# Start-up of a pooling-mixer trunk: who evicts the first fold, where the row factors stand, which queue stores the first block, and when the later weights are formed

## The chip, the cores and the metric

The kernel runs on one core of a Trainium2 chip. The metric is the time on the device, in microseconds (us), as the median of several runs. One more execution of each kernel was recorded by the hardware profiler; all rows of a profile come from that one execution.

## What is computed

The reference runs one layer (DEPTH is 1), so only the pooling mixer is used, on 4096 tokens of width 1024 in float32:

```python
h = x
normed = rms_norm(h, norm_w)                    # over the 1024 channels
u, gate = split(normed @ pool_in_w, 2)          # 1024 -> 2 x 1024
ug = u in 4 groups of 256 channels
pooled[g] = trailing_mean(ug[g], (2, 4, 8, 16)[g]) - ug[g]
mixed[g] = pooled[g] @ group_w[g] + group_b[g]
h = h + (mixed * scale * silu(gate)) @ pool_out_w
return rms_norm(h, final_norm_w)
```

## The kernel before, in words

**Three stages.** Pooling is linear, so the group map is folded into the input weights first: `fold` multiplies a transposed slice of the value half of `pool_in_w` by `group_w` and scales the product by the norm weight. It is called for 4 chunks of rows in each of two halves q of the value columns. Stage "a" (4 blocks b of 1024 tokens) multiplies the normalised input by the folded weights of half q = 0, stage "b" by those of q = 1, both with the gate columns of their half; stage "o" multiplies by `pool_out_w`, adds x and does the final norm.

**Seven products for eight.** Each block's product is a 2 by 2 block product done with seven multiplications (Strassen-Winograd). They are called P1 to P7 and run in the order P1, P2, P6, P7, P5, P4, P3. Each is 48 matmuls in stage a. Their left and right sides are sums and differences of quarters: of the input ("11", "12", "21", "22"), and of the weights.

**Each float32 operand is split in two.** `split` makes a rounded high part on ScalarE (`copy`) and the rest on VectorE (`sub`), both as fp32r; `mm3` multiplies three of the four pairs. A product thus needs 4 operand tiles written by ScalarE and VectorE (the weights `w[i]`, kept for all blocks, and the operands `op0` to `op3`, two for each product, so that a product's operands are split while the product before it runs).

**The start.** This is where the change lies. TensorE warms up, folds half q = 0 (chunks 0 to 3), folds half q = 1, and begins the products of block 0. Meanwhile:

- `fold` ends with one eviction of a PSUM bank for each of two halves of a chunk, on ScalarE (L296), in both q. With the first half's results VectorE and ScalarE make the weights of P1 (`split_scaled`, L205/L206) and of P6 (`second_side`, L886).
- The row factors 1/rms of block 0 come in two halves of 512 tokens. ScalarE squares and sums 4 tiles of rows (`square_row`, L315), `stats` (L322, `rsqrt` L186 to L190) makes the factors, and `spread_rs` puts them across the partitions: a high and low part, two products with an identity tile on VectorE (L339, into the tile of the weights of P7), two matmuls with ones (L346), a copy into `rstd`. The input quarters are multiplied by `rstd` (`normalize`, L148).
- The results of the second fold are stored to DRAM (`wvd`, L895) from SyncE's queue, between the loads of the input. They are read back much later.
- `split_in` (L435) splits a product's operands and stores some of the quarters to DRAM for stage b (`sd`, L379), from ScalarE's queue. For P6 it also forms the quarter sum for P3 (`form_s4`).
- `rest_of_first` makes the weights of P5, P4 and P3 in the steps n = 2, 3 and 4 (P6, P7, P5) of the main loop, ahead of the forming and splitting of the operands of the steps to come.

**What sets the order.** The program is recorded in Python order and a scheduler places the instructions of each engine by priority; `tc.high_priority()` lifts what is recorded inside it, `tc.issue_after` holds a piece back. Each engine then runs its list strictly in order. A DMA takes one of 8 completion counters in turn, so that the ninth DMA of SyncE and ScalarE waits until the first of them has landed; DMAs that GpSimd issues have a set of 8 counters of their own. Buffers for quarters come from pools (`st`, `vt`, and the still unused weight tiles `early`, `early5`) by age; a buffer that is still being stored can't be written again.

Tiles of the start that the text below names: `op_85`, `op_86` hold P1's, P6's and P5's operands, `op_87`, `op_88` P2's, P7's and P4's. `vt_102`, `vt_103` are the quarter "12" of block 0, `st_93`, `st_94` the quarter "21", `vt_105`, `vt_106` the quarter "22", which is loaded last.

Of the kernel before, what the change touches and what calls it, by code (L numbers as in the profile page):

```python
# [12 lines left out]
AF = mybir.ActivationFunctionType  # L13
ALU = mybir.AluOpType
# [16 lines left out]
P1, P2, P3, P4, P5, P6, P7 = range(1, 8)  # L31
# [29 lines left out]
def kernel(  # L61
# [32 lines left out]
    nc = tc.nc  # L94
# [7 lines left out]
    banks = [psum.tile([P, H], F32, tag=f"bank{i}", name=f"bank{i}") for i in range(8)]  # L102
# [35 lines left out]
    def give(ap):  # L138
        next(p for p in (st, vt, early, early5) if id(ap) in p.used).give(ap)
# [13 lines left out]
    def split(dst, src):  # L153
# [5 lines left out]
    norm_c = [colt[:, k : k + 1] for k in range(NK)]  # L159
# [5 lines left out]
    wvd = [dram.tile([P, 2, H], F32, name=f"wvd{k}") for k in range(4)]  # L165
# [6 lines left out]
        for i in range(P1, P7 + 1)  # L172
    }
    sd = [
        {
            i: [dram.tile([P, 2, H], F32, name=f"sd{b}_{i}_{h}") for h in range(2)]
            for i in (P1, P2, P7, P4)
        }
        for b in range(NB)
    ]  # L180
# [100 lines left out]
            )  # L281
        return r

    def fold(q, k, g, r, ps2, o):

        for kk in range(2):
            for j in range(2):
                for t in range(2):
                    nc.tensor.matmul(  # L289
                        ps2[kk][:, j * 256 : (j + 1) * 256],  # L290
                        r[:, kk, 2 * j + t, :],
                        g[:, 2 * j + t, :],
                        start=(t == 0),
                        stop=(t == 1),
                    )
            last = nc.scalar.activation(o[:, kk], ps2[kk], AF.Copy, scale=norm_c[k + kk])  # L296
        give(r)
        return last

# [4 lines left out]
    def load_row(b, half, j, pool=None):  # L304
        row = b * TB + (1 - half) * H
        rows = x[row : row + H, :].rearrange("(p j) d -> p j d", j=4)
        u = take("p (a b) -> p a b", pool, a=1)
        nc.sync.dma_start(out=u[:, 0], in_=rows[:, j, :])
        held[b, half, j] = u
# [10 lines left out]
    def stats(b, half):  # L320
        ms = small.tile([P, 4], F32, tag="ms", name=f"ms{b}_{half}")
        nc.vector.tensor_scalar(  # L322
            out=ms, in0=sums[b, half], scalar1=1.0 / D, scalar2=EPS, op0=ALU.mult, op1=ALU.add
        )
        tmp = small.tile([P, 4], F32, tag="tmp", name=f"tmp{b}_{half}")
        rs = small.tile([P, 4], F32, tag="rs", name=f"rs{b}_{half}")
        rsqrt(rs, tmp, ms)
        return rs
# [4 lines left out]
    def spread_rs(half, rs):  # L333

        hl = small.tile([P, 2, 4], F32R, tag="hl", name=f"hl{half}")
        split(hl, rs)
        r = w[P7][0]
        for s in range(2):
            nc.vector.tensor_tensor(  # L339
                out=r[:, s, 0].rearrange("p (a j) -> p a j", j=4),  # L340
                in0=ident.rearrange("p a b -> p (a b)")[:, 0:P].unsqueeze(2).to_broadcast([P, P, 4]),
                in1=hl[:, s].bitcast(F32).unsqueeze(1).to_broadcast([P, P, 4]),
                op=ALU.mult,
            )
        for s in range(2):
            nc.tensor.matmul(  # L346
                banks[7], ones, r[:, s, 0], start=s == 0, stop=s == 1, skip_group_check=True
            )
        if half == 0:
            rstd[0] = take()  # L350
        copy(rstd[0][:, half], banks[7])
# [18 lines left out]
        turn[0] += 1  # L370
        return t.rearrange(pattern, **sizes)

    def split_halves(us, saved=None):
        ts = []
        for h, u in enumerate(us):
            t = next_op("p (s a b) -> p s a b", s=2, a=2)
            split(t, u)
            if saved is not None:
                nc.scalar.dma_start(out=saved[h], in_=u)  # L379
            ts.append(t)  # L380
        return ts

# [46 lines left out]
    def normalize_a2(b):  # L429
        for h in range(2):  # L430
            normalize(b, 1, xs[b]["21"][h])
            normalize(b, 1, xs[b]["22"][h])
        give(rstd.pop(b))

    def split_in(q, b, i):  # L435
        s = xs[b]
        key = {P1: "11", P2: "12", P6: "2", P7: "21", P5: "11", P4: "22", P3: "12"}[i]
        t = split_halves(s[key], None if q else sd[b].get(i))
        if i == P6:
            form_s4(b)  # L440
        if i not in (P1, P2, P6):
            for u in s.pop(key):
                give(u)
        return t

    def form_s4(b):
        for u, s2 in zip(xs[b]["12"], xs[b]["2"]):
            sub(u, u, s2)
# [335 lines left out]
    def form(n):  # L784
        kind, b, i = step(n)
        if kind in ("a", "b"):
            form_in(kind == "b", b, i)
# [15 lines left out]
    def run(n, between=None):  # L803
        kind, b, i = steps[n]
        sets = sets_of(kind, b)
        if kind == "o":
            product_out(i, split_up.pop(n), sets, n == len(steps) - 1)
            evict_o(b, i, sets)
        else:
            product_in(i, split_up.pop(n), sets, i == P1, between)  # L810
            evict_in(b, 0 if kind == "a" else 1, i, sets)
# [30 lines left out]
    gw, ru, g0 = [None] * 2, {}, []  # L842
# [15 lines left out]
    for n, (h, k) in enumerate(chunks):  # L858
        if k < 4:
            o = v0[h] = take(pool=early)  # L860
        else:
            o = v1[h] = take()
        fold(0, k, gw[0], ru[0, k], banks[2 * (n % 2) : 2 * (n % 2) + 2], o)
        if n == 0:
            ru[1, 0] = load_wut(1, 0)
            load(0)
        elif n == 1:
            for hh in range(2):
                split_scaled(w[P1][hh], g0[hh], pair(norm_c, hh, 0))
        elif n == 2:  # L870
            for j in range(4):
                square_row(0, 0, j)
            rs = stats(0, 0)
    give(gw[0])
    for h, k in chunks[1:]:
        ru[1, k] = load_wut(1, k)
# [15 lines left out]
    for n, (h, k) in enumerate(chunks):  # L892
        o = take(pool=early if n < 2 else early5)
        last = fold(1, k, gw[1], ru[1, k], banks[2 * (n % 2) : 2 * (n % 2) + 2], o)
        nc.sync.dma_start(out=wvd[k // 2], in_=o)  # L895
        give(o)
        if n == 0:
            spread_rs(0, rs)
            form(0)
            split_step(0)  # L900
            second_side(0)
        elif n == 2:
            behind = last.ins
    give(gw[1])
    load(2)
    with tc.issue_after(behind):
        for j in range(4):
            square_row(0, 1, j)
    rs = stats(0, 1)
    run(0, lambda: spread_rs(1, rs))  # L910
    give(ident)
    form(1)
    split_step(1)
# [44 lines left out]
    def advance(what, n, f, reach):  # L958
        while at[what] + 1 < len(steps) and at[what] + 1 <= n + reach(*steps[at[what] + 1]):
            at[what] += 1  # L960
            f(at[what])
# [20 lines left out]
    for n in range(2, len(steps)):  # L982
        kind, b, i = steps[n]
        ahead = kind == "a" and b + 1 < NB
        keep[0] = 5 if kind == "b" and b == NB - 1 else 3
        advance("load", n, load, load_reach)
        if ahead:
            rows, squares = row_plan(b)
            for half, rs in scales.items():
                store_rs(b + 1, half, rs)  # L990
                load_rstd(b + 1, half)
            scales.clear()
            for j in squares.get(i, ()):
                with tc.issue_after(evicted[0]):
                    square_row(b + 1, j // 4, j % 4)
                if j % 4 == 3:
                    scales[j // 4] = stats(b + 1, j // 4)
            for j in rows.get(i, ()):
                load_row(b + 1, j // 4, j % 4, early if b == 0 and i == P6 else None)
        if kind == "a" and b == 0:  # L1000
            rest_of_first(n)
        if kind == "a" and b > 0 and i == P1:
            normalize_a2(b)
        form(n + 2)
        advance("split", n, split_step, split_reach)
        pool_due(n)
        run(n)
        if kind in ("a", "b"):
            pool_later(n)
            if kind == "a":  # L1010
                pool_due(n)
            if b == NB - 1:
                load_w(wbd if kind == "a" else wod, i)
            if i == P5:
                if kind == "a" and b in (1, 2):
                    make_wb(b - 1)
                elif kind == "b" and b in (1, 2):
                    make_wo(b - 1)
            if kind == "b" and b == NB - 1 and i == P3:
                f = take("p (a b) -> p a b", a=2)  # L1020
                nc.sync.dma_start(
                    out=f.rearrange("p a b -> p (a b)"), in_=final_w.partition_broadcast(P)
                )
                fw.append(f)
# [52 lines left out]
```

## Time and profile before

| what | us |
|---|---|
| median of 3 runs (lowest, highest) | 977.49 (976.59, 979.3) |
| the profiled execution, whole | 976.22 |
| its span, first to last instruction | 974.4 |
| TensorE busy in the span | 952.1 |
| VectorE busy | 741.5 |
| ScalarE busy | 456.7 |

The profile has these views, used below: the page (busy time of each engine), the waits (which line of an engine waited for what, in total, how often, the longest), the timeline of one engine (start, us, engine, line, operation, tiles, count, and in brackets the idle time before with what ended it), the groups of instructions (busy us, mean ns of one), and windows (busy time and DMA traffic in stretches). In a timeline, a group "x48" spans all of its instructions. Tiles are named there without their numbers. Instructions of VectorE and ScalarE overlap by about 0.1 us: two of 1.23 us take 2.36.

### The profile page before, as it was taken

The numbers are of one execution on the slowest core, as the hardware profiler recorded it, in microseconds if no ns is written. First come the engines' busy times: TensorE is split into PE (matmuls) and PEld (weight loads), VectorE is DVE, ScalarE is ACT, GpSimd is POOL, SyncE is SP. The second block draws the span as 40 slices with busy tenths as digits, with TensorE's granted clock in tenths as the row PEclk, the third lists the DMA queues.
The fourth block names the chain that finished last, engine by engine and source line by source line (L and its number), as shares of the span: only waits on it lengthen the run. The fifth ranks groups of instructions, "written<-read, shape, count | busy, mean of one in ns | idle before, by whom it ended". The sixth has DMA issues, their size and how long they took to land.

```text
span 974.4 us, 11068 instructions
## 1 busy us (share of the span) xinstructions
PE 952.1 (98%) x4190; PEld 786.3 (81%) x4190; DVE 741.5 (76%) x899; ACT 456.7 (47%) x687; POOL 0.2 (0%) x4
## 2 busy tenths in 40 slices
PE   8898999999999999999999999999999999999996
PEld 7777888878877888888888888888888888888885
DVE  3688893887699694497598499589987677677675
ACT  6658447437455454335444535553414324334333
POOL 0000000000000000000000000000000000000000
PEclk9999999999999999999999999999999999999999
DMA  9985675877885624114704723645646446356022
GB/s 336 369 313 152 229 262 168 323 270 237 316 289 205 230 104 153 44 43 152 302 34 145 274 89 130 223 163 181 224 161 236 118 164 216 109 195 214 23 87 87
DMA packets 68933, 184.35 MB, mean 189 GB/s; under 512 B 6928, under 2 KB 24464, under 8 KB 68880
## 3 DMA queue, kind: packets, MB, share of 16 engines
q1 hardware_dynamic: 63552, 165.81, 49.1%
q10 hardware_dynamic: 5328, 17.84, 4.6%
q8 instruction: 33, 0.54, 0.2%
q14 instruction: 20, 0.16, 0.1%
HBM read 116.50 MB, written 67.12 MB: 188 GB/s over the span
## 4 chain that ended last, share of the span: by engine, by line
PE 83%; DVE 6%; DMA 6%; ACT 3%; issue 1%; SPq 0%
PE bank L455 81%; DMA rd<-rs 1%; PE bank L289 1%; DMA st<-rd 1%; DMA vt<-in_xt 1%; DMA wbd<-vt 1%; DMA wbd<-st 1%; DVE w L145 1%; DVE op L145 1%; DVE vt L148 1%; DVE vt L145 1%; ACT st L315 1%; PE bank L835 1%; DVE vt L142 1%; DVE st L145 1%
## 5 line engine op out<-in xcount | busy, mean ns | idle before, releaser
L455 PE MATMUL bank<-op,w 128*128 128x512 f32 x2688 | 612.4, 390 | 9.3 <-DVE op L145 5.9
L455 PEld LDWEIGHTS bank<-op,w 128*128 128x128 f32 x2688 | 503.9, 188 | 117.2 <-DVE op L145 8.0
L455 PE MATMUL bank<-w,op 128*128 128x512 f32 (+1 forms) x1356 | 305.0, 387 | 0.0
L455 PEld LDWEIGHTS bank<-w,op 128*128 128x128 f32 x1356 | 253.0, 188 | 52.0
L151 ACT ACTIVATE op<-st 128x1024 fp32r<-128x1024 f32 x121 | 127.5, 1056 | 144.7 <-PE bank L455 116.2
L145 DVE TENSOR_TENSOR op<-st,op 128x1024 fp32r<-128x1024 f32 x121 | 147.2, 1223 | 58.8 <-ACT op L151 58.5
L142 DVE TENSOR_TENSOR vt<-vt 128x1028 f32<-128x1028 f32 (+6 forms) x72 | 88.1, 1235 | 1.1 <-DMA wbd<-vt 0.9
L151 ACT ACTIVATE op<-vt 128x1024 fp32r<-128x1024 f32 x45 | 47.6, 1058 | 73.2 <-PE bank L455 64.0
L142 DVE TENSOR_TENSOR st<-bank,st 128x512 f32<-128x512 f32 x76 | 51.9, 688 | 35.5 <-PE bank L455 33.3
L151 ACT ACTIVATE vt<-bank 128x512 f32<-128x512 f32 x94 | 54.8, 594 | 39.8 <-PE bank L455 33.7
L142 DVE TENSOR_TENSOR vt<-bank,vt 128x512 f32<-128x512 f32 (+1 forms) x85 | 57.0, 680 | 15.1 <-PE bank L455 8.7
L145 DVE TENSOR_TENSOR op<-vt,op 128x1024 fp32r<-128x1024 f32 x45 | 55.0, 1223 | 16.8 <-ACT op L151 16.6
L145 DVE TENSOR_TENSOR w<-st,w 128x1024 fp32r<-128x1024 f32 x32 | 39.1, 1225 | 23.7 <-ACT w L151 23.4
L151 ACT ACTIVATE w<-st 128x1024 fp32r<-128x1024 f32 x32 | 33.7, 1058 | 36.6 <-PE bank L455 28.7
L151 ACT ACTIVATE bank<-bank 128x512 f32<-128x512 f32 x48 | 27.9, 582 | 45.0 <-PE bank L455 32.5
L145 DVE TENSOR_TENSOR st<-st,st 128x1024 f32<-128x1024 f32 x38 | 46.2, 1224 | 2.7 <-issue 1.4
L148 DVE TENSOR_TENSOR st<-st,st 128x1024 f32<-128x1024 f32 (+1 forms) x22 | 25.4, 1174 | 22.0 <-DMA st<-rd 20.7
L151 ACT ACTIVATE st<-bank 128x512 f32<-128x512 f32 x36 | 20.7, 596 | 21.7 <-PE bank L455 10.4
L536 DVE SCALAR_TENSOR_TENSOR vt<-vt,vt 128x1024 f32<-128x1024 f32 x24 | 29.4, 1227 | 0.1
L289 PE MATMUL bank<-early,early 128*128 128x256 f32 x128 | 28.2, 380 | 1.1 <-ACT st L315 1.1
L289 PEld LDWEIGHTS bank<-early,early 128*128 128x128 f32 x128 | 24.3, 191 | 4.8 <-ACT st L315 1.5
L142 DVE TENSOR_TENSOR st<-st,st 128x1024 f32<-128x1024 f32 x21 | 25.4, 1227 | 0.1
(105 smaller groups left out, 407.9 us busy)
## 6 DMA issues: line engine op xcount, KB each, us to landing
st<-in_x SPq DMA_DIRECT2D x32, 512.0 KB, 4.4
st<-sd SPq DMA_DIRECT2D x29, 512.0 KB, 4.7
vt<-in_x SPq DMA_DIRECT2D x27, 512.0 KB, 5.0
st<-in_xt SPq DMA_DIRECT2D x20, 512.0 KB, 5.4
sd<-st ACTq DMA_DIRECT2D x20, 512.0 KB, 6.5
st<-yd SPq DMA_DIRECT2D x19, 512.0 KB, 3.8
yd<-st SPq DMA_DIRECT2D x17, 512.0 KB, 3.0
out<-st SPq DMA_DIRECT2D x17, 512.0 KB, 4.6
```

The source lines that it names most:

```text
L142: nc.vector.tensor_tensor(out=dst, in0=a, in1=b, op=ALU.add)
L145: nc.vector.tensor_tensor(out=dst, in0=a, in1=b, op=ALU.subtract)
L148: nc.vector.tensor_tensor(out=dst, in0=a, in1=b, op=ALU.mult)
L151: return nc.scalar.activation(dst, src, func)
L289: nc.tensor.matmul(ps2[kk][:, j * 256 : (j + 1) * 256], r[:, kk, 2 * j + t, :], g[:, 2 * j + t, :], start=(t == 0), stop=(t == 1),)
L315: nc.scalar.activation(u[:, 0], u[:, 0], AF.Square, accum_out=sums[b, half][:, j : j + 1])
L455: nc.tensor.matmul(ps, a, b, start=start and n == 0, stop=stop and n == 2, skip_group_check=True)
L536: nc.vector.scalar_tensor_tensor(out=s[:, :, at : at + H], in0=s[:, :, at : at + H], scalar=1.0 / win, in1=v[:, :, HIST:], op0=ALU.mult, o ...
L835: nc.tensor.matmul(banks[4 + c % 4], warm[:, 0:P], warm, start=True, stop=True, skip_group_check=True)
```

## The change

Five edits, all in the start:

1. The evictions of the first fold (q = 0) go to VectorE, as a `tensor_scalar` multiplication by the same column.
2. `stats` and `spread_rs` of block 0 are recorded under `tc.high_priority()`, in both halves; the first `spread_rs`, with the forming and splitting of P1's operand and the first `second_side`, is recorded after the second chunk of the second fold (n == 1) in place of the first.
3. The stores of the second fold (`wvd`) are issued by GpSimd in place of SyncE.
4. The stores of block 0's quarters (`sd`) are issued by GpSimd in place of ScalarE.
5. In the main loop at n = 2, the splitting of P7's operand comes first, then `form_s4` of block 0 and the forming for P5, and only then `rest_of_first`; at later n `rest_of_first` also stands behind forming and splitting. `normalize_a2` keeps its place ahead of them.

```diff
-    def fold(q, k, g, r, ps2, o):
+    def fold(q, k, g, r, ps2, o, on_vector=False):
...
-            last = nc.scalar.activation(o[:, kk], ps2[kk], AF.Copy, scale=norm_c[k + kk])
+            if on_vector:
+                last = nc.vector.tensor_scalar(
+                    out=o[:, kk], in0=ps2[kk], scalar1=norm_c[k + kk], scalar2=None, op0=ALU.mult
+                )
+            else:
+                last = nc.scalar.activation(o[:, kk], ps2[kk], AF.Copy, scale=norm_c[k + kk])
...
-                nc.scalar.dma_start(out=saved[h], in_=u)
+                (nc.gpsimd if by_pool else nc.scalar).dma_start(out=saved[h], in_=u)
...
-        t = split_halves(s[key], None if q else sd[b].get(i))
-        if i == P6:
+        t = split_halves(s[key], None if q else sd[b].get(i), b == 0)
+        if i == P6 and (q or b):
             form_s4(b)
...
-        fold(0, k, gw[0], ru[0, k], banks[2 * (n % 2) : 2 * (n % 2) + 2], o)
+        fold(0, k, gw[0], ru[0, k], banks[2 * (n % 2) : 2 * (n % 2) + 2], o, True)
...
-            rs = stats(0, 0)
+            with tc.high_priority():
+                rs = stats(0, 0)
...
-        nc.sync.dma_start(out=wvd[k // 2], in_=o)
+        nc.gpsimd.dma_start(out=wvd[k // 2], in_=o)
         give(o)
-        if n == 0:
-            spread_rs(0, rs)
+        if n == 1:
+            with tc.high_priority():
+                spread_rs(0, rs)
...
-    rs = stats(0, 1)
-    run(0, lambda: spread_rs(1, rs))
+    with tc.high_priority():
+        rs = stats(0, 1)
+
+    def spread_second():
+        with tc.high_priority():
+            spread_rs(1, rs)
+
+    run(0, spread_second)
...
-        if kind == "a" and b == 0:
-            rest_of_first(n)
         if kind == "a" and b > 0 and i == P1:
             normalize_a2(b)
-        form(n + 2)
+        if n > 2:
+            form(n + 2)
         advance("split", n, split_step, split_reach)
+        if n == 2:
+            form_s4(0)
+            form(n + 2)
+        if kind == "a" and b == 0:
+            rest_of_first(n)
```

## The prediction, on record before the changed kernel ran

> **What bounds the kernel now.** First the page, for the share of each engine; then the waits of TensorE over the whole run.
>
> ```profile
> PE 952.1 (98%) x4190; PEld 786.3 (81%) x4190; DVE 741.5 (76%) x899; ACT 456.7 (47%) x687; POOL 0.2 (0%) x4
> ...
> PE bank L455 <- DVE op L145: 5.9, 5, 3.3
> PE bank L346 <- DVE w L339: 2.8, 1, 2.8
> PE bank L455 <- ACT op L151: 2.3, 2, 1.6
> PE bank L835 <- DVE op L833: 1.4, 1, 1.4
> PE bank L289 <- ACT st L315: 1.1, 1, 1.1
> PE bank L455 <- ACT bank L151: 1.1, 1, 1.1
> ```
>
> TensorE is busy 952.1 of the span's 974.4 us. The change takes no matmul away, so it can win only from the 22.3 us in which TensorE stands. 14.6 us of them are the six waits here; the rest is the last eviction and store, which is not touched. Where the waits lie is read from TensorE's timeline of the start:
>
> ```profile
> 7.47 13.97 PE L289 MATMUL bank<-early,early 128*128 128x256 f32 x64
> 22.54 3.69 PE L289 MATMUL bank<-early,early 128*128 128x256 f32 x16 [1.10 <-ACT st L315]
> 29.06 1.10 PE L346 MATMUL bank<-w,w 128*128 128x512 f32 x2 [2.83 <-DVE w L339]
> 30.01 10.52 PE L289 MATMUL bank<-early,early 128*128 128x256 f32 x48
> 40.18 7.40 PE L455 MATMUL bank<-op,w 128*128 128x512 f32 x31
> 47.42 0.39 PE L346 MATMUL bank<-w,w 128*128 128x512 f32 x1
> ...
> 48.10 0.39 PE L346 MATMUL bank<-w,w 128*128 128x512 f32 x1
> 48.32 14.44 PE L455 MATMUL bank<-op,w 128*128 128x512 f32 x63
> 64.40 1.21 PE L455 MATMUL bank<-op,w 128*128 128x512 f32 x4 [1.63 <-ACT op L151]
> 66.29 11.17 PE L455 MATMUL bank<-op,w 128*128 128x512 f32 x48 [0.68 <-ACT op L151]
> 80.78 1.45 PE L455 MATMUL bank<-op,w 128*128 128x512 f32 x5 [3.32 <-DVE op L145]
> ```
>
> Two places count. Ahead of the first spread (29.06) TensorE stands 1.10 + 2.83 = 3.93 us: **stall A**. Before P6 (64.40, 66.29) and P7 (80.78) it stands 1.63 + 0.68 + 3.32 = 5.63 us: **stall C**. Between them, at the second spread (47.42, 48.10), it does not stand: **place B**. The remaining 3.7 us of the waits lie after 200 us, in stages the change does not edit.
>
> **Edit 1, half of the evictions to VectorE, and edit 2, the first factors: stall A.** VectorE's and ScalarE's timelines, and the waits of that stretch:
>
> ```profile
> 25.24 0.75 DVE L886 SCALAR_TENSOR_TENSOR st<-st,colt,early 128x512 f32<-128x512 f32 x1
> ...
> 27.11 1.22 DVE L145 TENSOR_TENSOR w<-st,w 128x1024 fp32r<-128x1024 f32 x1 [0.65 <-ACT w L151]
> ...
> 28.32 1.29 DVE L339 TENSOR_TENSOR w<-early,hl 128x512 fp32r<-128x512 f32 x2
> 26.02 1.06 ACT L151 ACTIVATE w<-st 128x1024 fp32r<-128x1024 f32 x1 [1.62 <-DVE st L886]
> L296 ACT ACTIVATE early<-bank,colt 128x512 f32<-128x512 f32 x12 | 7.9, 681 | 6.5 <-PE bank L289 6.4
> L142 DVE TENSOR_TENSOR vt<-bank,vt 128x512 f32<-128x512 f32 (+1 forms) x85 | 57.0, 680 | 15.1 <-PE bank L455 8.7
> L206 DVE SCALAR_TENSOR_TENSOR w<-st,colt,w 128x512 fp32r<-128x512 f32 x6 | 4.2, 750 | 11.9 <-ACT w L205 11.9
> ```
>
> No row shows a `tensor_scalar` from PSUM on VectorE. The nearest, L142 from a bank, is 0.68 us; one SBUF operation on 512 columns is 0.75; I take 0.69. Eight of them put 5.5 us on VectorE, which idles 11.9 us there behind L205, and take 8 x 0.681 = 5.4 us off ScalarE. But the first factor isn't bound by ScalarE's evictions alone. In the changed program's order VectorE does, from the last bank of the fold on (7.47 + 13.97 = 21.44): eviction 0.69, the low part of P6's first weights 1.14 (two of these take 2.36, so one step is 1.14), the mean (0.1), the difference for the second weights 1.14, reciprocal (0.1), two L886 steps 1.33 and the small steps: 26.0. That is where the last L886 ends now (25.24 + 0.75 with the factor's small steps between). From there the chain is unchanged: ScalarE's high part of those weights (26.02 to 27.08), VectorE's low part, only then the high and low part of the factor and L339. High priority has not lifted the factor past these weights. So **stall A stays**, within 0.4 us either way; the 1.10 before it merges with it. One fold matmul (two records of 13.97 / 64 = 0.22 us) now stands between the two spread matmuls, which take 1.10 for 2 x 0.39, and fills 0.3 us of that gap: **-0.3**.
>
> **Place B, the second factor.** ScalarE's and VectorE's rows:
>
> ```profile
> 42.19 1.05 ACT L315 ACTIVATE vt<-vt 128x1024 f32<-128x1024 f32 x1
> 43.14 0.19 ACT L315 ACTIVATION_READ_ACCUMULATOR vt<-vt 128x1 f32 x1
> 43.80 0.20 ACT L186 ACTIVATE tmp<-ms 128x4 f32<-128x4 f32 x1
> 46.19 1.29 DVE L339 TENSOR_TENSOR w<-early,hl 128x512 fp32r<-128x512 f32 x2
> ```
>
> Now the last square ends at 43.3 and TensorE has the factor at 47.4. In the new order more stands in the chain: ScalarE's high part of `op_87` (0.95) before the square root, which ends at 44.6; VectorE's low part of `op_87` until 45.6, reciprocal and two small steps to 46.2, low part of `op_88` 1.14, two low parts of P2's weights 0.66 each around the last small steps, then the factor's low part: L339 at 49.0 to 50.2, 2.7 later. TensorE's spread matmul now stands behind 38 of P1's matmuls, not 31: at 14.44 / 63 = 0.229 each it is reached at 40.18 + 38 x 0.229 = 48.9. It waits to 49.6 and the second to 50.2, with one matmul between: **+0.9 us of new wait**. Behind it in TensorE's queue stand P1's last 9 and P2; nothing else waits for them. If the cover of the 7 further matmuls were gone, it would be 2.5.
>
> **Edits 3 and 4, stores from GpSimd: the loads.** SyncE's waits and timeline, DMA windows (us, busy of each engine, clock, DMA share, GB/s), the chain, and the wait on `vt_103`:
>
> ```profile
> SPq L199 <- DMA sd<-st: 8.4, 1, 8.4
> 39.69 3.62 SPq L895 DMA_DIRECT2D wvd<-early  x4
> 28.00:32.00 4.00, 2.83 (x12) 2.24 (x13) 2.71 (x5) 0.92 (x2) 0.00 (x0) 1.00 1.03 410
> 36.00:40.00 4.00, 4.00 (x20) 3.51 (x20) 2.45 (x2) 2.97 (x6) 0.00 (x0) 1.00 0.85 342
> 40.00:43.40 3.40, 3.40 (x17) 2.82 (x16) 0.12 (x2) 3.40 (x8) 0.00 (x0) 1.00 0.79 263
> 46.48 11.70 DMA vt<-in_xt
> 38.27 1.23 DVE L148 TENSOR_TENSOR vt<-vt,st 128x1024 f32<-128x1024 f32 x1 [0.67 <-DMA vt<-in_xt]
> sd<-st ACTq DMA_DIRECT2D x20, 512.0 KB, 6.5
> ```
>
> SyncE stood 8.4 us at a load because its counter belonged to a quarter's store that ScalarE had issued late; then came four `wvd` issues, 3.62 us. Both leave SyncE's queue, and the last quarter's four loads are issued some 12 us sooner. They do not land 12 us sooner: the same 4 MB of stores stay ahead in traffic, and DMA runs at 410 GB/s when full. What is won is the hole: (68 x 4.0 + 147 x 3.4) / 410 = 1.9 us. The last load, landed at 46.48 + 11.70 = 58.18, comes at about 56.3, the one before it (512 KB, 1.28 us) at 55.0. ScalarE's 8 issues cost it nothing on the path.
>
> **Edit 5 and stall C.** VectorE's rows before P6:
>
> ```profile
> 54.56 2.36 DVE L148 TENSOR_TENSOR st<-st,st 128x1024 f32<-128x1024 f32 x2
> ...
> 65.02 2.36 DVE L145 TENSOR_TENSOR op<-early,op 128x1024 fp32r<-128x1024 f32 x2
> 79.49 2.37 DVE L145 TENSOR_TENSOR op<-st,op 128x1024 fp32r<-128x1024 f32 x2
> ```
>
> The last row is P7's operand, now behind P5's weights and P4's sums (65.02 to 79.49): the 3.32 us. In the new order it stands beside P6's. After L339 at 50.2: P2's second weights 1.32, P7's first weights 1.14, so the second quarters' `normalize` starts at 52.7, not 54.56. Four of these, four sums, P7's second weights, the low parts of `op_87` and `op_85`: 11 x 1.14 = 12.5, to 65.3 if no load is late. `vt_105` would be wanted at 53.8 and lands at 55.0: +1.2, so 65.4 for `op_87` and 66.5 for `op_85`. TensorE leaves P2 at 48.32 + 14.44 + 0.9 = 63.7, does P6's first 4 matmuls (0.9), waits 0.8 for `op_87`, does 4, and waits 0.3: **1.1 us in place of 5.63** (0 with early loads; 3.0 if the last load still lands at 58.18, which puts all 1.9 us later). P7's second half (`op_88`, 2.3 us after `op_87`) is wanted 11 us later. Late next are P5's operand and weights, moved behind: four more operations of 1.14 (`form_s4`, P5's sums), then P5's weights (four steps of 1.14 and two pairs of 0.66, 7.2 in all), then `op_85`, ready at about 82; TensorE wants it 21.9 us after P6's start, at 86.7. Cover 5 us.
>
> **Sum.** -0.3 (A) + 0.9 (B) - 5.63 + 1.1 (C) = **-3.9 us**. The profiled execution, 976.22 (974.4 and 1.8 around), goes to 972.3. It lies 1.27 below the median of 977.49, so the median goes to **973.6**.
>
> **Rivals.** (1) *The stores crowd the loads.* For: the last quarter's loads and the stores are now in flight together from about 29 us on. Against: DMA is full (1.03) now as well. Place: VectorE's mean for the second factor stands behind `normalize` of `vt_103`, now landed at 38.25. It is needed by 43.4 - 1.2 = 42.2. Three `wvd` ahead of it, served first, are 3 x 1.28 = 3.8 us: 42.1, the edge. Every us beyond is one of TensorE's at B. At 2.4 us beyond, the gain is 1.5: **976.0**, no change. The Trainium skill ("DMA: Bandwidth & Descriptors", section "Issuing engines are not separate DMA queues") says that transfers of all issuing engines end on the same 16 engines and interleave. That is this rival; the 410 GB/s agree.
>
> (2) *GpSimd's stores come out slowly*, the slower side. GpSimd has 12 DMAs in one queue and issued none before. VectorE's `form_s4` writes into `vt_102` and `vt_103` at 67.7 (52.7 + 13 x 1.14), which must be stored by then; they are ready at 38 to 42 us, and such a store takes 6.5 us now. It decides from 67.7 + 5 (cover) = 73 on. Were they issued only when VectorE pauses, they would land after 67.7 + 6.5 = 74, `st_93` (P6's eviction waits for its store) 6.5 later, behind it on ScalarE P5's weights: some 8 us, **981.6** (973.6 + 8). The Trainium skill ("SBUF — State Buffer", section "SBUF: two separate sides") warns of just this: a DMA from GpSimd waits while VectorE holds their common port in a two-port mode. Its section "Who interferes with whom" narrows it: operations with two SBUF inputs take only the read side. The rows between 28 and 66 us are nearly all TENSOR_TENSOR and SCALAR_TENSOR_TENSOR, so by the second sentence little is lost; no row here shows a DMA from GpSimd.
>
> (3) *The factors come sooner than worked out* (evictions shorter than 0.69, small steps between): stall A down by up to 0.4, B and C to nothing, later waits less: up to 6.5 us, **971.0**.
>
> **How the numbers follow.** Of this kernel's time, 0.3% (2.9 us) can be told from no change: 974.6 and 980.4 are the bounds. The forecast with rival 3 has 0.63 (of that rival 3: 0.08), all faster; rival 1, gains of 0 to 2.9, 0.28; rival 2 and other losses 0.09. The range runs from 970.8 (a little beyond rival 3) to 977.5 (a gain of nothing), leaving out rival 2 and a little on either side.
>
> **What would show it.** In the new profile: the first L346 still at 29 to 29.5 with about 4 us of wait (else A is wrong); a wait of 0.5 to 1.5 us at the second L346, near 50 (over 2: rival 1); at P6 at most 3 us in all, and none at P7; the last `vt` load landed at 55 to 57; GpSimd's stores of `vt_102` and `vt_103` landed before 60 (after 70: rival 2). The forecast is wrong if waits beyond 100 us grow from 3.7 to over 6.

## The result: 972.25 us, and the profile after

| what | before | after |
|---|---|---|
| median of 4 runs each (lowest, highest), us | 977.93 (976.59, 979.3) | 972.25 (971.78, 973.14) |
| after as a share of before, 95% interval | | 0.9952 [0.9935, 0.9969] |
| the profiled execution; its span, us | 976.22; 974.4 | 973.14; 971.0 |
| TensorE's waits up to 135 us; from there to 303 us | 11.00; 3.67 | 6.24; 5.47 |

The changed kernel is faster by 0.5%; the interval leaves out 1. The ratio here and those further down are as recorded with the runs; the quotient of the two medians is 0.9942 (5.7 us) and lies within the interval. The prediction said 973.6, from 970.8 to 977.5. The last row adds up the bracketed idle times of TensorE's timeline, the opening 1.4 us included; after 303 us TensorE waits no more in either kernel. The page and the waits of after:

```profile
PE 951.5 (98%) x4190; PEld 786.4 (81%) x4190; DVE 745.6 (77%) x907; ACT 452.2 (47%) x679; POOL 6.7 (1%) x16
...
PE bank L460 <- DVE op L145: 4.7, 4, 2.1
PE bank L351 <- DVE w L344: 3.5, 2, 2.9
```

TensorE's busy time is the same (952.1 before); VectorE has the eight evictions, GpSimd its twelve DMA issues. The wait of 2.3 us behind ScalarE's operands is gone from the list. Where the rest lies is read from TensorE's timeline:

```profile
22.38 3.69 PE L289 MATMUL bank<-early,early 128*128 128x256 f32 x16 [1.10 <-DVE st L297]
29.00 0.50 PE L351 MATMUL bank<-w,w 128*128 128x512 f32 x1 [2.94 <-DVE w L344]
29.34 0.59 PE L289 MATMUL bank<-early,early 128*128 128x256 f32 x2
...
39.74 9.00 PE L460 MATMUL bank<-op,w 128*128 128x512 f32 x38
49.29 0.50 PE L351 MATMUL bank<-w,w 128*128 128x512 f32 x1 [0.56 <-DVE w L344]
...
50.23 78.99 PE L460 MATMUL bank<-op,w 128*128 128x512 f32 x346
129.40 66.95 PE L460 MATMUL bank<-op,w 128*128 128x512 f32 x294 [0.18 <-DVE op L145]
...
198.24 12.30 PE L460 MATMUL bank<-op,w 128*128 128x512 f32 x53 [1.89 <-DVE op L145]
211.50 74.00 PE L460 MATMUL bank<-op,w 128*128 128x512 f32 x325 [0.96 <-ACT bank L151]
287.56 11.18 PE L460 MATMUL bank<-op,w 128*128 128x512 f32 x48 [2.06 <-DVE op L145]
```

The reader is to see three things. Stall A is there as before (1.10 + 2.94). Place B has a small new wait, 0.56. And the row "x346" runs from 50.23 to 129 us without a bracket: both P6 and P7 lie in it, so stall C is gone whole. The waits near 200 and 290 us are longer than they were.

VectorE's timeline shows why C is gone:

```profile
52.22 1.22 DVE L148 TENSOR_TENSOR st<-st,st 128x1024 f32<-128x1024 f32 x1
53.55 1.23 DVE L148 TENSOR_TENSOR vt<-vt,st 128x1024 f32<-128x1024 f32 x1
...
55.83 1.22 DVE L148 TENSOR_TENSOR vt<-vt,st 128x1024 f32<-128x1024 f32 x1
...
62.64 1.22 DVE L145 TENSOR_TENSOR op<-st,op 128x1024 fp32r<-128x1024 f32 x1
63.78 2.36 DVE L145 TENSOR_TENSOR op<-early,op 128x1024 fp32r<-128x1024 f32 x2
66.05 1.22 DVE L145 TENSOR_TENSOR op<-st,op 128x1024 fp32r<-128x1024 f32 x1
...
79.13 1.22 DVE L145 TENSOR_TENSOR op<-st,op 128x1024 fp32r<-128x1024 f32 x1
```

The four `normalize` follow each other with no load in brackets: the loads of the last quarter (L393) have landed. The last of them, in after (its issue, and the time from there to its landing), puts that at 36.0 + 18.8 = 54.8 us, 3.3 us sooner than before (58.18):

```profile
L393 SPq DMA_DIRECT2D vt<-in_xt x1: 328/328/328, 36.0 to 36.0; - x1
...
DMA to landing us min/median/max: 18.8/18.8/18.8
```

The first row of `op<-st` (62.64) is `op_87`, P7's operand: TensorE's list has four of P7's matmuls behind the first four of P6, so it is the first low part that is needed there, and it is ready at 63.86. P7's second one (66.05) now also stands beside P6's, not at 79.49. What moved behind it, P5's operand, is the row at 79.13: early enough, since no wait follows.

The stores from GpSimd: the issues (column after the bar: busy us, mean ns) and their landing (KB, median us from issue to landing), then the two stretches in which DMA was not full before:

```profile
L901 POOL DMA_DIRECT2D wvd<-early x4 | 2.3, 565 | 33.1 <-ACT early L301 31.2 <-DMA vt<-in_xt 1.9
L384 POOL DMA_DIRECT2D sd<-vt x4 | 2.1, 533 | 15.2 <-DVE vt L148 14.9 <-issue 0.3
```

```profile
wvd<-early POOLq DMA_DIRECT2D x4, 512.0 KB, 7.7
sd<-st POOLq DMA_DIRECT2D x4, 512.0 KB, 6.6
sd<-vt POOLq DMA_DIRECT2D x4, 512.0 KB, 7.5
```

```profile
36.00:40.00 4.00, 4.00 (x20) 3.51 (x20) 1.23 (x1) 3.33 (x7) 1.06 (x2) 1.00 1.03 413
40.00:43.40 3.40, 3.40 (x17) 2.78 (x16) 1.36 (x3) 3.40 (x7) 1.07 (x2) 1.00 1.03 415
```

The hole is filled (342 and 263 GB/s before), and the stores land in 6.3 to 9.6 us (the medians are 6.6 to 7.7); the median of `sd<-st` from ScalarE's queue, over the whole kernel before, is 6.5. A second stretch, which the prediction did not count, was not full before either; before, then after:

```profile
48.00:52.00 4.00, 4.00 (x20) 3.30 (x19) 2.39 (x4) 2.44 (x5) 0.00 (x0) 1.00 1.00 362
```

```profile
48.00:52.00 4.00, 3.44 (x15) 2.34 (x14) 3.53 (x6) 3.71 (x7) 0.00 (x0) 1.00 1.03 419
```

The new wait at B is read from the chain of work (start, length, what) in that stretch:

```profile
29.77 17.83 DMA st<-in_in_w
...
47.62 0.72 ACT w L205
48.35 0.10 ACT hl L151
...
48.47 0.16 DVE hl L145
48.63 0.61 DVE w L344
...
49.29 0.50 PE bank L351
```

The second factor's high part (`hl`, ScalarE) stands behind the scaling of P2's second weights (L205), and that waits for their load until 47.6. The prediction had put the whole wait on VectorE's list. That load was issued 9.5 us sooner than before (29.77, not 39.22) and yet landed 4 us later (47.60, not 43.61): it is now in flight together with the stores, and without them (ns, below) it lands at 40.4.

### The profile page after: what moved, and what is told of

It reads as the page before. It is cut to its first block, busy times and chain, and to the rows that moved or that the text cites. A ratio compares the mean times of both kernels' runs of the same rounds, so it can differ in the third digit from the quotient of the medians.

```text
span 971.0 us, 11079 instructions
## 1 busy us (share of the span) xinstructions
PE 951.5 (98%) x4190; PEld 786.4 (81%) x4190; DVE 745.6 (77%) x907; ACT 452.2 (47%) x679; POOL 6.7 (1%) x16
## 4 chain that ended last, share of the span: by engine, by line
PE 75%; DMA 10%; DVE 8%; ACT 4%; issue 1%; SPq 0%; ACTq 0%; DVEq 0%
PE bank L460 73%; DMA st<-in_in_w 3%; DMA rd<-rs 2%; DMA st<-rd 2%; DVE op L145 2%; PE bank L289 1%; DMA wbd<-vt 1%; DVE vt L142 1%; ACT vt L320 1%; DVE st L145 1%; DVE st L148 1%; DMA wbd<-st 1%; DMA early<-in_wut 1%; DVE st L546 1%; DVE vt L148 1%
## 5 line engine op out<-in xcount | busy, mean ns | idle before, releaser
L151 ACT ACTIVATE vt<-bank 128x512 f32<-128x512 f32 x94 | 54.8, 594 | 35.8 <-PE bank L460 34.2
```

The source lines that it names most:

```text
L151: return nc.scalar.activation(dst, src, func)
```

## The experiments

The theory after the first comparison: the order (edit 5) carries most of the gain, the stores (3, 4) the rest, the evictions and priorities (1, 2) nothing. Its rivals: the stores carry it; the evictions carry it. Each ratio is to the kernel before on the same chip. Waits are sums of the brackets of TensorE's timeline, "half clock" the stretches of 3.4 us ahead of 303 us in which the windows show a granted clock of 0.50 (in g1 the two are one stretch of 6.8).

| kernel | ratio [95%] | waits to 135 us | 135 to 303 us | half clock |
|---|---|---|---|---|
| before | 1 | 11.00 | 3.67 | none |
| after, first profile | 0.9952 [0.9935, 0.9969] | 6.24 | 5.47 | none |
| c_after (after again) | 0.9943 [0.9920, 0.9965] | 5.90 | 3.96 | none |
| u1: edit 1 undone | 0.9942 [0.9929, 0.9955] | 5.40 | 2.41 | 1 |
| u12: edits 1, 2 undone | 0.9933 [0.9916, 0.9949] | 5.55 | 1.77 | none |
| u34: edits 3, 4 undone | 0.9949 [0.9936, 0.9962] | 6.88 | 2.47 | none |
| u5: edit 5 undone | 0.9982 [0.9968, 0.9995] | 8.95 | 3.13 | 2 |
| o5: edit 5 alone | 0.9964 [0.9949, 0.9978] | 7.71 | 2.52 | 3 |
| o34: edits 3, 4 alone | 0.9973 [0.9958, 0.9988] | 8.03 | 4.39 | 2 |
| f2 | 0.9937 [0.9923, 0.9951] | 7.39 | 3.78 | 1 |
| f5 | 0.9939 [0.9917, 0.9961] | 7.51 | 3.97 | none |
| f6 | 0.9936 [0.9921, 0.9950] | 5.67 | 4.48 | 1 |
| ns: no first stores | 0.9929 [0.9913, 0.9945] | 5.66 | 2.89 | 1 |
| g1 | 0.9952 [0.9937, 0.9967] | 6.69 | 2.05 | 2 |

**c_after**, the changed kernel again, as a measure for the others.

> The changed kernel as it is, on the chip of the next three, as their measure. The first comparison gave 0.9952 [0.9935, 0.9969]; the same is expected, between 0.9935 and 0.9965. Before 130 us its profile should repeat: about 4 us of waits at the first spread, 0.6 at the second, none ahead of P6 and P7. The waits between 190 and 305 us added up to 5.7 us in its first profile and to 2.4 to 3.8 us in the profiles of the variants; if they are chance, this run can show any sum from 2.4 to 5.7.

Measured: 971.48 against 977.23 us, 0.9943. The waits up to 135 us repeat (5.90 against 6.24), those from 135 to 303 do not: 3.96 against 5.47. So of the growth from 3.67 to 5.47 in the first profile 1.5 us differ between two executions of one kernel; what is left, 0.3, is no cost that can be told.

**u1_scalar_evicts**, edit 1 undone:

```diff
-        fold(0, k, gw[0], ru[0, k], banks[2 * (n % 2) : 2 * (n % 2) + 2], o, True)
+        fold(0, k, gw[0], ru[0, k], banks[2 * (n % 2) : 2 * (n % 2) + 2], o)
```

> The changed kernel with the first fold's evictions back on ScalarE. Theory 1 (VectorE's order before P6 and P7, then the loads, make the gain): the first factor is bound by the chain behind the last bank, which is no shorter on either engine, so the first spread stays at 29 us and only the matmul between the two spread matmuls moves: 0.3 to 0.5 us slower than the changed kernel, no wait at P7. Theory 2 (the stores from GpSimd are the gain): the same, no change. Theory 3 (ScalarE, freed of eight evictions of 0.68 us, is the gain): 3 to 5 us slower than the changed kernel, about 976 to 977.

Measured: 969.77 against 976.11 us, 0.9942. Stall A is 1.69 + 2.25 = 3.94 us, after's 4.04: who evicts the first fold doesn't matter to it. At B there is no wait. The 3 to 5 us that theory 3 said would be lost are not lost: that ScalarE, freed of the evictions, makes the gain is refuted.

**u12_only_345**, edits 1 and 2 undone: u1's line, and `stats` and both `spread_rs` without `tc.high_priority()`, the first again at n == 0.

> The changed kernel with edits 1 and 2 undone: what is left is the order (5) and the stores (3, 4). Theory (order and stores carry the gain, evictions and priorities nothing that can be seen): 0.993 to 0.997 of before, as the changed kernel (0.9943 and 0.9952), with the wait ahead of P7 gone and those ahead of P6 at most 1.2 us together. Rival (the priorities give the last microsecond; with 5 alone the waits ahead of P6 were 2.3 us, and with 1, 2 and 5 they were 1.2 us): the waits ahead of P6 come back to 2 us or more, and the time is 0.9965 to 0.9980.

Measured: 970.79 against 977.2 us, 0.9933, with stall A at 0.97 + 2.96 and no wait at B or P6. The rival falls: nothing that can be seen is lost without edits 1 and 2. Their part in the gain can't be told from zero; the intervals leave room for a loss of some 2 us.

**u34_hw_stores**, edits 3 and 4 undone:

```diff
-                (nc.gpsimd if by_pool else nc.scalar).dma_start(out=saved[h], in_=u)
+                nc.scalar.dma_start(out=saved[h], in_=u)
...
-        nc.gpsimd.dma_start(out=wvd[k // 2], in_=o)
+        nc.sync.dma_start(out=wvd[k // 2], in_=o)
```

> The changed kernel with the stores of the second fold back on SyncE and the first block's stores back on ScalarE. Theory 1: the last loads land 2 to 3 us later again, the waits before P6 come back to 1.5 to 2.5 us in all, none at P7: 1.5 to 2 us slower than the changed kernel, about 974. Theory 2: the whole gain goes, about 977.5. Theory 3: no change.

Measured: 970.75 against 976.11 us, 0.9949. Small waits come back (0.22 for P2's weights, 0.28, 0.24 and 0.48 at P6), 1.2 us together, and at 130 us TensorE is 1.5 us behind after. Its time can't be told from after's. With the other edits in place the stores are worth some 1.5 us by the profile at 130 us, and nothing that shows in the time.

**u5_old_order**, edit 5 undone:

```diff
-        if i == P6 and (q or b):
+        if i == P6:
             form_s4(b)
...
+        if kind == "a" and b == 0:
+            rest_of_first(n)
...
-        if n > 2:
-            form(n + 2)
+        form(n + 2)
...
-        if n == 2:
-            form_s4(0)
-            form(n + 2)
-        if kind == "a" and b == 0:
-            rest_of_first(n)
```

> The changed kernel with the later weights (rest_of_first) ahead of forming and splitting again, and form_s4 back in the splitting of P6's operand. Theory 1: the wait at P7 comes back, 2.5 to 3.3 us, none at P6: about 975. Theory 2 and theory 3: no change, 972.3.

Measured: 974.36 against 976.11 us, 0.9982. The wait ahead of P7 is back; TensorE's row, then VectorE's:

```profile
78.81 51.57 PE L460 MATMUL bank<-op,w 128*128 128x512 f32 x219 [2.58 <-DVE op L145]
```

```profile
77.54 2.35 DVE L145 TENSOR_TENSOR op<-st,op 128x1024 fp32r<-128x1024 f32 x2
```

The low parts of P7's operand are made from 77.5 to 79.9, behind P5's weights, as before. Undoing this edit takes back 0.0030 to 0.0039 of the time, 3 to 4 us.

**o5_order_alone** and **o34_stores_alone**, the kernel before with edit 5 alone, and with edits 3 and 4 alone (the diffs above, the other way).

> The kernel before with edit 5 alone. Theory A, now the first (the order carries the gain, and what the stores add is not seen in the time): the wait of 3.32 us ahead of P7 is gone, those ahead of P6 (1.63 and 0.68) stay or go, and the time is 0.9940 to 0.9965 of before, within 1.5 us of the changed kernel. Theory B (the edits add up: about 2.5 us from the order and 1.5 to 2 us from the stores that have left SyncE's and ScalarE's queues): the waits ahead of P6 stay at about 2.3 us together, and the time is 0.9970 to 0.9980, 1.5 to 2 us behind the changed kernel.

> The kernel before with edits 3 and 4 alone (all of the first block's stores from GpSimd). Theory A: the loads land sooner and the waits ahead of P6 (2.3 us) shrink, but the wait ahead of P7 stays at 2.6 to 3.3 us and takes back what they gave; the time is 0.9985 to 1.0005 of before. Theory B: the same profile up to P7, with the time at 0.9975 to 0.9985.

Measured: o5 973.57, 0.9964; o34 975.17, 0.9973 (before 977.23). TensorE's waits in o5, then in o34:

```profile
65.34 1.20 PE L455 MATMUL bank<-op,w 128*128 128x512 f32 x4 [1.63 <-ACT op L151]
67.23 133.13 PE L455 MATMUL bank<-op,w 128*128 128x512 f32 x579 [0.70 <-ACT op L151]
```

```profile
78.33 52.04 PE L455 MATMUL bank<-op,w 128*128 128x512 f32 x221 [2.50 <-DVE op L145]
```

The two halves of stall C have different owners. The order takes away P7's 3.32 us and leaves P6's 2.3; the stores take away P6's, since the loads land sooner (VectorE's first `normalize` of the last quarter's stretch starts at 52.84, not 54.56), and leave 2.50 at P7. By the times o5 lies at the edge of theory A's range and o34 in neither range, next to B's; the rows fit what both theories said. Together o5's 0.0036 and o34's 0.0027 make 0.0063, where all five edits gave 0.0048 and 0.0057: within the noise the two parts add up, as theory B has it. With edits 1, 2 and 5 the stores' part is smaller: u34 keeps 1.0 us at P6 and not o5's 2.3.

**ns_no_first_stores**: after, with the stores themselves left out.

```diff
+    rows = lambda k: in_w[2 * k * P : (2 * k + 2) * P, 0:H].rearrange("(t p) c -> p t c", p=P)
+    wvd = [rows(k) for k in range(4)]
+    sd[0] = {i: [rows(h) for h in range(2)] for i in sd[0]}
...
-            if saved is not None:
+            if saved is not None and not by_pool:
...
-        nc.gpsimd.dma_start(out=wvd[k // 2], in_=o)
```

> The changed kernel without the twelve stores of edits 3 and 4; what is loaded back from them later is read from in_w in their place, so the output is not the reference's. Theory (the loads end ahead of what waits for them in the changed kernel, so the stores that share the DMA queues with them cost nothing now): the last loads of xt land 3 to 5 us sooner, the waits of the tensor engine up to 130 us stay within 1 us of the changed kernel's, and the time is within 1 us of it, 0.993 to 0.9955 of before. Rival (the stores crowd the loads, and the factors and P2's weights wait for them): the waits at the two spreads fall from 4.5 to under 3 us and the time to 0.992 or less.

Measured: 970.44 against 977.2 us, 0.9929, just below the range; its interval overlaps after's. DMA moved 131 GB/s from 50 to 58.2 us in place of 412, and the last load of the quarter landed at 45.6, not 54.8: 9 us sooner, more than the 3 to 5 that were said. Yet stall A is 1.50 + 2.53 = 4.03; only the 0.56 at B is gone. What is left at the start doesn't hang on the stores.

**f2_factor_first**: after, with `second_side(1)`'s VectorE part queued behind the first factor's products.

```diff
-                spread_rs(0, rs)
+                made = spread_rs(0, rs)
...
-    second_side(1)
+    with tc.issue_after(made):
+        second_side(1)
```

> The changed kernel with VectorE's part of P6's second weights (second_side(1)) queued behind the first factor's products. Theory 1: the first spread comes at 25 to 26 us in place of 29, so the wait there falls from 4.0 us (both pieces) to 1.1 to 2.5; TensorE then reaches the second spread and P6 earlier, where the loads and VectorE are late: 0.7 to 1.5 us at the second spread, 0.5 to 1.5 at P6. Net 0.5 to 1.5 us faster than the changed kernel, 971 to 972. Rival: the first wait is set by a load and not by the factor's chain, then the spread stays at 29 and nothing changes. Second rival: all that is won at the first spread is kept, 969.

Measured: 969.79 against 976.11 us, 0.9937. The first spread comes at 25.51 in place of 29.00; but the second waits 2.40 us. TensorE's row, then ScalarE's:

```profile
50.24 0.79 PE L351 MATMUL bank<-w,w 128*128 128x512 f32 x1 [2.40 <-DVE w L344]
```

```profile
48.57 0.72 ACT L205 ACTIVATE w<-st,colt 128x512 fp32r<-128x512 f32 x1 [1.75 <-DMA st<-in_in_w]
49.20 0.19 ACT L151 ACTIVATE hl<-rs 128x4 fp32r<-128x4 f32 x1
```

A is 1.91 + 1.62 = 3.53, 0.5 us less than in after, and B 1.84 more: what was won at A, and more, is waited for at B, behind the load of P2's second weights.

**f5_both_second** adds to f2 that P2's weights are scaled behind the second factor, on both engines:

```diff
-        split_scaled(w[P2][h], g1[h], pair(norm_c, h, 1))
+        for j, c in enumerate(pair(norm_c, h, 1)):
+            with tc.issue_after(second[0]):
+                nc.scalar.activation(w[P2][h][:, 0, j], g1[h][:, j], AF.Copy, scale=c)
+            with tc.issue_after(second[1]):
+                nc.vector.scalar_tensor_tensor(
+                    out=w[P2][h][:, 1, j], in0=g1[h][:, j], scalar=c,
+                    in1=w[P2][h][:, 0, j].bitcast(F32), op0=ALU.mult, op1=ALU.subtract,
+                )
```

(`second[0]` is the high part of the second factor, `second[1]` the last of its products.)

> The changed kernel with second_side(1) held behind the first factor's products, as in f2_factor_first, and now P2's second weights too, their scaling on ScalarE behind the second factor's high part and their remainder on VectorE behind its products. Theory A (the second factor waited in f2 for the high part, which stood on ScalarE behind the load of P2's second weights): the 2.40 us at the second spread fall under 0.5, the 1.62 at the first stays near 1.6, and P2, whose weights are now late by at most 1 us, starts without a wait; at 130 us the kernel stands some 4 us ahead of the changed one, and the time is 0.990 to 0.9935 of before unless the waits after 190 us take more. Rival (the factor itself comes late, from its squares and its root): the wait at the second spread stays over 1.5 us, and the time stays at f2's, 0.9937.

Measured: 972.03 against 977.23 us, 0.9939. The wait at B falls to 0.92, not under 0.5, and a third place opens: VectorE's row, then TensorE's:

```profile
52.30 1.23 DVE L148 TENSOR_TENSOR st<-st,st 128x1024 f32<-128x1024 f32 x1 [1.48 <-DMA st<-in_xt]
```

```profile
63.48 1.42 PE L462 MATMUL bank<-op,w 128*128 128x512 f32 x5 [0.95 <-ACT op L151]
65.80 64.46 PE L462 MATMUL bank<-op,w 128*128 128x512 f32 x283 [0.89 <-DVE op L145]
```

VectorE reaches the last quarter's loads sooner, waits for them, and P6 waits for VectorE. A is 1.53 + 1.76 = 3.29, 0.75 us less than in after; at B and P6 it waits 2.76 in place of 0.56. More came back than was won: at 130 us the kernel is about 1 us behind after, where theory A had it 4 us ahead.

**f6_high_before_weights**: after, with the second half of P2's weights behind the second factor's high part on ScalarE, and nothing else.

```diff
-    for h in range(2):
-        split_scaled(w[P2][h], g1[h], pair(norm_c, h, 1))
+    split_scaled(w[P2][0], g1[0], pair(norm_c, 0, 1))
+    with tc.issue_after(second[0]):
+        split_scaled(w[P2][1], g1[1], pair(norm_c, 1, 1))
```

> The changed kernel with one move: ScalarE scales P2's second half of weights behind the second factor's high part, where it stood between them. Theory (the second spread's 0.4 to 0.6 us are this load): the wait at the second spread is gone or under 0.15 us, ScalarE's high part no longer stands behind a DMA, the waits at the first spread and ahead of P6 stay as they are, and the time is within 0.6 us of the changed kernel, which is not to be told from it. Rival (the root of the squares is late itself): the wait stays between 0.4 and 0.9 us.

Measured: 970.56 against 977.2 us, 0.9936. ScalarE's rows, then TensorE's at B:

```profile
48.32 0.20 ACT L151 ACTIVATE hl<-rs 128x4 fp32r<-128x4 f32 x1 [0.42 <-DVE rs L148]
48.95 1.34 ACT L205 ACTIVATE w<-st,colt 128x512 fp32r<-128x512 f32 x2 [0.42 <-DMA st<-in_in_w]
```

```profile
49.68 0.50 PE L352 MATMUL bank<-w,w 128*128 128x512 f32 x1
```

No bracket at B, and the load's wait now lies behind `hl`, where nobody waits for it. TensorE and the factor both come 0.9 to 1.0 us later here than in after, so the missing bracket alone would say little; but `hl` starts 0.04 us behind the end of `rs`, where it stood 0.95 us behind it in after (48.25 against 47.30). That is more than B's 0.56 us, and its cause is shown; half a microsecond is too little to be seen in the time, as expected.

**g1_scalar_and_held**: f2 with edit 1 undone as well.

> f2_factor_first with edit 1 undone as well, the two variants whose medians were lowest (0.9937 and 0.9942, neither to be told from the changed kernel's 0.9943 and 0.9952). Theory (a wait taken away ahead of 60 us comes back at the next place that hangs on the same loads, on ScalarE or on VectorE): the waits up to 130 us add up to 5.5 to 7.5 us, as in the changed kernel and in f2, and the time is 0.9925 to 0.9950 of before. Rival (the two add up): at most 4.5 us of waits and 0.9925 or less.

Measured: 972.24 against 977.2 us, 0.9952, just above the range; 6.69 us of waits. The two do not add up. Of all these kernels only u5 stands clear of both measurements of after in the time (by 0.0030 and 0.0039), o34 of the second alone and barely, o5 of neither; f2, f5, f6 and g1 can't be told from after. As far as the time shows, u12 does with edits 3 to 5 what all five do.

## Why the prediction was right, point by point

- **Stall A stays: right.** 3.93 before, 4.04 after; 3.94 with the evictions on ScalarE. The eviction from a bank on VectorE took 0.75 us, not 0.69, but one step of it 0.66; neither reaches TensorE. One fold matmul stands between the spread matmuls, as said: it is the row at 29.34, whose "x2" are its two records.
- **Place B, +0.9: right in kind, wrong in cause, too dear.** 0.56 and 0.42. The step that failed is the chain at B: VectorE had L344 ready at 48.55 to 49.84 (49.0 to 50.2 said), and it waited for ScalarE's `hl`, which stood behind the load of P2's second weights, a row that the prediction's chain does not have. f6 shows it.
- **Loads 1.9 us sooner: right in kind, the term too small.** The last two landed at 53.53 and 54.84 (55.0 and 56.3 said; 56.81 and 58.18 before), 3.3 us sooner. The term counted the hole up to 43.4 us alone, and DMA had moved only 362 GB/s from 48 to 52 us as well.
- **Rival 1, the stores crowd the loads: half true.** The loads issued beside the stores did land later than before: `vt_103` at 40.42 (38.25), P2's second weights at 47.60 (43.61). But `vt_103` was needed by 42.2 and was there 1.8 us ahead of that. Without any stores (ns) the spreads wait no less than 4.0 us, so crowding cost 0.5 us at most, the wait at B.
- **Stall C, 5.63 to 1.1: mechanism right, term too dear.** It is 0. `op_87` was there at 63.86, not 65.4: the wait of 1.2 us for `vt_105` shrank to a pause of 0.2 ahead of 53.55, since it landed at 53.53 and not at 55.0, and VectorE started 0.5 earlier (52.22, not 52.7). The term that was mis-sized is thus the landing of the loads. P5's operand (ready at 80.35; 82 said) cost nothing.
- **Which edit carries what: the division held.** The prediction gave P7's 3.32 us to the order, and to the loads the sooner start of P6's operands. o5 and o34 show that.
- **Rival 2, GpSimd's stores come out slowly: false.** They land in 6.3 to 9.6 us. `vt_102` and `vt_103` were stored by 47.3 and 52.3 (issued at 39.47 and 42.73, and 7.8 and 9.6 us to land), long before VectorE writes into them at 67.19. The Trainium skill ("SBUF — State Buffer", section "Who interferes with whom") says in its narrower sentence that operations with two SBUF inputs take only the read side. The trace agrees: VectorE was busy 8.08 of 8.20 us with such operations from 50 to 58.2 us, and GpSimd's two issues there took 0.53 us each, as they did from 36 to 40 us, where VectorE was busy 1.23 of 4.00.
- **The sum.** Waits up to 135 us were to fall by 3.6 us (5.63 - 1.1 - 0.9) and fell by 4.8 (5.1 in c_after). The waits after 200 us were taken as unchanged; in the profile of after they took 1.8 back, in c_after 0.3. Profile against profile the gain is 3.1 and 4.95 us; -3.9 had been said. So two terms were off, B by 0.3 and C by 1.1 us, both to the same side. That the first profile gained 3.1 and not 4.95 is the chance of the waits after 200 us, which took back what the two terms had left out. The medians differ by 5.7; the last section has what is known of the rest.

## What to carry to other kernels

Follow a stall to each of its halves: the 5.6 us at P6 and P7 looked like one, and one half belonged to a list on VectorE, the other to a load's queue. Before giving an operation priority on one engine, look at the other engine in its chain: the factor's high part stood behind a DMA on ScalarE, and raising VectorE's part could not help. And where three places hang on the same loads and the same VectorE, time taken from the first is waited for at the second and third (f2, f5), so count the sum of waits, not the stall that went.

## What the runs showed of the hardware that was not expected

**A stall of about 2 us can cost 1.7 us more.** In eight of the fourteen profiles the granted clock falls to half after a stall, for 3.4 us (in g1 for twice that). In u1 TensorE stood 2.25 us; its row, then the windows behind it (the last three columns: granted clock, DMA share, GB/s):

```profile
1.46 5.46 PE L840 MATMUL bank<-op 128*128 128x512 f32 x14 [1.46 <-DVE op L838]
...
28.36 1.10 PE L351 MATMUL bank<-w,w 128*128 128x512 f32 x2 [2.25 <-DVE w L344]
```

```profile
26.00:29.00 3.00, 0.64 (x3) 0.23 (x2) 2.50 (x4) 1.62 (x4) 0.67 (x1) 1.00 1.03 393
29.00:30.00 1.00, 1.00 (x4) 0.85 (x5) 0.00 (x0) 0.44 (x1) 0.00 (x0) 0.83 1.02 406
30.00:33.00 3.00, 3.00 (x8) 2.37 (x8) 2.81 (x3) 1.63 (x3) 0.69 (x2) 0.50 1.02 411
33.00:34.00 1.00, 1.00 (x5) 0.86 (x5) 0.76 (x1) 1.00 (x2) 0.38 (x1) 0.97 1.04 426
```

0.17 + 3 x 0.50 + 0.03 = 1.70 us of clock are lost, that is 3.4 us at half, beginning at 29.66. Before, after, c_after, u12 and u34 stood longer at the same place (2.83 to 3.19 us) and lost nothing. What tells them apart is their warm-up, the 14 matmuls at the very start (f2, f5 and g1, whose first spread comes elsewhere, are left out):

| kernel | warm-up, us | the wait before the first spread | half clock from |
|---|---|---|---|
| o34 | 4.99 | 2.17 | 28.6 |
| u5 | 5.10 | 2.28 | 28.9 |
| f6 | 5.11 | 2.14 | 28.8 |
| u1, o5 | 5.46 | 2.25, 2.37 | 29.7 |
| ns | 5.63 | 2.53 | 30.0 |
| after, u34, u12, before, c_after | 6.00 to 6.20 | 2.83 to 3.19 | never |

The longer the warm-up, the later the half clock begins, twice as much later: a warm-up that is 0.64 us longer (ns against o34) puts it off by 1.4. That is what a window of 3.4 us would do which runs on its own and judges TensorE at its ends: it ends the slow start of the warm-up, and some 24 us later the stall falls whole into one window or is cut by a window's end.

The traces' records of the granted clock bear it out. In u1 they begin with full clock at 5.76 us, within the warm-up, and the half clock comes at 29.66, that is 23.89 or 7 x 3.413 us later. It is 7 windows in all six profiles of the table that have it (5 in g1, 13 in f2). If the first 303 us of all fourteen profiles are cut into such windows, TensorE stood 1.95 us or more in 13 of them, and a window of half clock followed each time; in every other window it stood 1.91 us or less, and none followed. Before's 2.83 us, from 26.23 to 29.06, are cut at 27.80 into 1.57 and 1.26. The Trainium skill ("TensorE: Matmul & The Clock Gate", section "Part 1: The HAM clock gate (the "warmup" mystery)") states such a window, free-running, of 3413 ns; the 3.4 us agree. It speaks of an idle window ahead of the slow state; here 1.95 us of standing within one were enough.

So where the windows lie differs from execution to execution (the warm-up is 6.00 and 6.20 us in two profiles of the changed kernel), and each stall of about 2 us or more costs 1.7 us more in some of them. The same was seen at P6 and near 202 us in o5, at P7 in u5 and o34, at B in f2 and at A in g1. Ahead of 100 us before has three such places (A, P6, P7), after one. That would make the change worth more in the medians (5.7 us) than between two profiles without half clock (3.1 and 4.95). Two executions speak for it: o5's profiled one, with three stretches of half clock, was the slowest of its twelve (975.54; median 973.57), and f2's, with one, the slowest of its five (972.51; the others 968.86 to 970.01). The mean granted clock of every other execution is on record too. Of the 23 executions of before beside c_after, the six at 0.997 or 0.998 span 972.8 to 974.3 us, the seven at 0.993 or 0.994 976.2 to 979.8: the longer ones are those that lost clock. On average before is at 0.9954 there, c_after at 0.9963, which is 4.5 and 3.6 us lost (the half clock behind the last matmul, which every profile has, included). Of the 5.4 us between their mean spans 0.9 are thus clock and 4.5 are not. With six executions of c_after the 0.9 is not clear of noise, and no run was made for it.

**The shorter warm-up gains nothing.** Where it ends sooner, TensorE waits the longer ahead of 22.4 us (1.5 to 1.9 us, not 0.8 to 1.1), in f2, f6 and o34 by name for the load of the fold's weights.
